# A one-core fp32 layer: weight-sum copies issued by another engine, a product's order, an eviction order, and two banks for the last block

## The chip, the cores and the metric

The kernel runs on one core of a Trainium2 chip. The metric is the device time of one execution in microseconds (us). A core has a tensor engine (PE, with its weight loads shown apart as PEld), a vector engine (DVE), a scalar engine (ACT), GpSimd (POOL) and a sync engine (SP), which mostly issues DMA transfers. Each engine takes its instructions in order and waits on semaphores for the others; transfers run on 16 DMA engines that all issuers share. Two of the DMA queues matter: q1, filled by SP and ACT, and q0, filled by POOL.

## The reference

One layer of a diffusion backbone over 1024 tokens of 1024 channels, all in fp32:

```python
hx = _modulate(_rmsnorm(x, norm1_g[l]), sh1, sc1)          # and hc, 256 context tokens
o_na  = _na_latent(...)                                    # neighbourhood attention + context keys
o_ret = _ret_output(_bi_retention(...), xrg)               # chunked retention, both directions
    # step: scores = (q k^T) * dmat ; out = scores v + (q state) * xi
    #       state = g_chunk * state + (k*zeta)^T v         (context tokens give the first state)
x = x + g1 * _merge(o_na, o_ret, xga, xgb, w_proj_na, w_proj_ret, w_out)
hx2 = _modulate(_rmsnorm(x, norm2_g[l]), sh2, sc2)
u = conv3(hx2 @ w_up) + conv_b ; a, val = split(u)          # 2 x 2816 columns
x = x + g2 * ((silu(a) * val) @ w_down)                    # 2816 -> 1024
return _rmsnorm(x, final_norm_g)
```

## The kernel before

**Products.** Every fp32 product is three products of a faster format: each operand is split into a high part (a cast, on ACT, line 95) and a low part (the rest, a subtraction, mostly on DVE, line 96), and PE multiplies hi by hi, hi by lo and lo by hi into one bank. `mm3` (L129 to L132) does this for one product, `open3` (L1421 to L1423) for one of a chain.

**The feed-forward part** uses a scheme with seven block products in place of eight. For that, sums of quarter blocks are needed, of the weights and of the activations. The up products run in units (class `Seven`, L1425), of 7 steps each; a unit's weight sums s1 to s4 are made on POOL (L1432 to L1435), cast on ACT and used by PE.

The down product is seven passes in a row: A11·B11, S2·T2, A12·B21, S3·T3, S1·T1, A22·T4, S4·B22, each over 11 steps j (a step is one `operands` pair, L2268, and 12 matmuls of 128x512 outputs, `steps`, L2289). The A and S are 512-column pieces of the activations, kept in DRAM as `d_a`; the T are sums of blocks of the down weights, kept in DRAM as `d_w`. They are made while the up products run:

- The activations: `conv` writes A11, A22, A12 and first copies of the S with SP's stores `d_a<-at` (L1981 and, for the second half of the blocks, L1986). Then POOL's accumulating transfers (`act_sum`, L1993, `d_a<-d_a`) do S3 += A11, S1 += A22, S2 += S1, S4 += S2 for each j, each after the one before it that it reads has landed.
- The weights: `block_sums` (L555) yields 88 calls for 11 jobs of 4 sums: 44 copies from the weights to `d_w` (`copy_of`, L560, transfers of 16x4096 elements issued by SP at L562) and 44 accumulating transfers on POOL (`sum_of`, L564, issued at L558). The order within a round is copy 0 of job n, sum 0 of job n-1, copy 2, sum 3 of job n-2, copy 1, sum 2 of n-1, copy 3, sum 1 of n-1. A sum waits for its copy; sum 1 waits for sum 0, and sum 3 for sum 1.

Both are put into the stream of the up units by hand: after steps 1 and 3 of a unit, `puts` (L592) has POOL copy one column of a result of that unit (`pad<-pu`, L593), which holds POOL until the step is there, then come two calls of `block_sums` and one of `act_sum`. What is left after the last unit is drained: first all of `block_sums`, then all of `act_sum` (L2250 to L2252). `late` keeps these instructions in program order; a scheduler places the others.

**Loads of the down product.** All operands of all passes are one stream of loads on SP's queue (`ur_load`, L2145 to L2147; 12 buffers, 8 loads ahead): `ur<-d_a` and `ur<-d_w` or `ur<-in_w_down`. A load waits for the sum it reads and holds every later one on SP. The copies L562 stand on SP between these loads and the activation stores.

**Retention.** For each of 4 heads, `front` computes q, k, v of a block of 128 tokens (blocks 0 and 1 are the context) into a bank, which is evicted: v's high part by ACT (L1165), its low part by DVE (L1166), and for context blocks k (`r`) by ACT (L1170). `state` scales k to `kz` (ACT L1199, DVE L1200) for the product dS. In `mix_a`, the product Q of q with two running states SS is one `mm3` (L1245); SS's high part is cast on ACT (L1230) and its low part made on POOL (L1231).

**The end.** In the last pass (p = 6), the first 7 of 11 steps are run for four blocks b = 0 to 3 together; the last four are run block by block under a written-out order (L2375 to L2404), each block ending with a scale and a subtraction on DVE (L2392, L2393), a sum of squares on ACT (L2395), a factor on POOL (L2310, L2311), a scaling on ACT and DVE (L2316, L2317) and a store. Block 3 does this in two halves of 256 columns, one after the other, in the same bank.

Of the kernel before, what the change touches and what calls it, by code (L numbers as in the profile page):

```python
# [8 lines left out]
F32 = mybir.dt.float32  # L9
F32R = mybir.dt.float32r  # L10
AF = mybir.ActivationFunctionType
ALU = mybir.AluOpType
# [4 lines left out]
P = 128  # L17
D = 1024
# [4 lines left out]
NCB = C // P  # L23
# [17 lines left out]
def tile_hybrid_layer(ctx, tc: tile.TileContext, io, dbg=None):  # L41
# [87 lines left out]
    def mm3(out, ah, al, bh, bl, first, last):  # L129
        pe.matmul(out, ah, bh, start=first, stop=False)  # L130
        pe.matmul(out, ah, bl, start=False, stop=False)  # L131
        pe.matmul(out, al, bh, start=False, stop=last)  # L132
# [419 lines left out]
    NH, EARLY, PRE = NF // 2, 4, 8  # L552
    seq = [j + NH * i for j in range(NH) for i in range(2)]

    def block_sums(jobs):  # L555

        def add(out, src):
            late(pool.dma_start(out, src, accum_op=ALU.add, max_dma_last_dim=8192))  # L558

        def copy_of(n, c):  # L560
            d, x, y, z, w = jobs[n]
            late(sync.dma_start(d[c], (y, z, z, w)[c]))  # L562

        def sum_of(n, c):  # L564
            d, x, y, z, w = jobs[n]
            add(d[c], (x, d[0], y, d[1])[c])

        jobs = list(jobs)
        for n in range(len(jobs) + 2):
            for f, m, c in ((copy_of, n, 0), (sum_of, n - 1, 0), (copy_of, n, 2), (sum_of, n - 2, 3), (copy_of, n, 1), (sum_of, n - 1, 2), (copy_of, n, 3), (sum_of, n - 1, 1)):  # L570
                if 0 <= m < len(jobs):
                    yield f(m, c)
# [14 lines left out]
    def down_jobs(j0, j1):  # L587
        for j in range(j0, j1):
            b = {(r, c): io["w_down"][c, NH * r + j] for r in range(2) for c in range(2)}
            yield [d_w[j, c] for c in range(4)], b[0, 0], b[0, 1], b[1, 1], b[1, 0]  # L590
# [539 lines left out]
    class Head:  # L1130
# [21 lines left out]
        def front(self, i):  # L1152

            src, tb = (hcp, i) if i < NCB else (hxp, self.order[i - NCB])
            c0 = P if i < NCB else 0
            m = mm_tile()
            for n, kb in enumerate(self.kbs):
                xh, xl = src(0, kb, tb * P, P), src(1, kb, tb * P, P)
                w = self.wr[kb]
                mm3(m[:, c0:512], xh, xl, w[:, 0, c0:512], w[:, 1, c0:512], n == 0, n == KB - 1)  # L1160
                if n in (2, 5):
                    yield
            vtag = f"c{i}" if i < NCB else tb
            self.v[i] = v = rt.tile([P, 2, DV], F32R, tag=f"v{vtag}", bufs=1, name="v")
            act.copy(v[:, 0], m[:, 256:512])  # L1165
            vec.tensor_tensor(v[:, 1], m[:, 256:512], v[:, 0].bitcast(F32), ALU.subtract)  # L1166
            r0 = rt.tile([P, 2, 2, 2, 32], F32, tag="r0", bufs=2, name="r0")
            self.r0[i] = r0f = r0.rearrange("p q a t i -> p q (a t i)")
            if i < NCB:
                act.copy(r0f[:, 1], m[:, P : 2 * P])  # L1170
                return
            r1 = rt.tile([P, 2, 2, 2, 32], F32, tag="r1", bufs=2, name="r1")
            mv = m[:, 0:256].rearrange("p (q a t i) -> p q a t i", q=2, a=2, t=2)
            for a, ti in ((0, tb), (1, NTB)):
                cs = cosT[:, ti, 0].unsqueeze(1).unsqueeze(1).to_broadcast([P, 2, 2, 32])
                sn = cosT[:, ti, 1].unsqueeze(1).to_broadcast([P, 2, 32])
                vec.tensor_tensor(r0[:, :, a], mv[:, :, a], cs, ALU.mult)
                vec.scalar_tensor_tensor(r1[:, :, a, 0], mv[:, :, a, 1], -1.0, sn, ALU.mult, ALU.mult)
                vec.tensor_tensor(r1[:, :, a, 1], mv[:, :, a, 0], sn, ALU.mult)
            pool.tensor_tensor(r0f, r0f, r1.rearrange("p q a t i -> p q (a t i)"), ALU.add)  # L1180
# [43 lines left out]
        def mix_a(self, n):  # L1224
            tb = self.back[n]
            q, k = self.qk[tb][:, :, 0], self.qk[tb][:, :, 1]
            run = self.run
            SS = rt.tile([P, 2, 2, DV], F32R, tag="SS", bufs=1, name="SS")
            for i, s in ((self.ci, self.sts[tb]), (self.oi, run)):
                act.copy(SS[:, 0, i], s)  # L1230
                pool.tensor_tensor(SS[:, 1, i], s, SS[:, 0, i].bitcast(F32), ALU.subtract)  # L1231
            if n + 1 < NTB:
                self.run = rt.tile([P, DV], F32, tag="run", bufs=2, name="run")
                vec.scalar_tensor_tensor(self.run, run, self.dec(4 + self.oi), self.dss[tb], ALU.mult, ALU.add)
            Ap = prt.tile([P, 2, P], F32, tag="s", bufs=2, name="Ap")
            pe.matmul(Ap, k[:, 0], q, start=True, stop=False, skip_group_check=True)
            pe.matmul(Ap[:, 0], k[:, 1], q[:, 0], start=False, stop=True, skip_group_check=True)
            A0 = rt.tile([P, 2, P], F32, tag="A0", bufs=1, name="A0")
            self.A[n] = A = rt.tile([P, 2, P], F32R, tag="Ahl", bufs=2, name="A")
            vec.tensor_tensor(A0, Ap, Dm[:, self.h].unsqueeze(1).to_broadcast([P, 2, P]), ALU.mult)  # L1240
            vec.tensor_tensor(A0[:, 0], A0[:, 0], A0[:, 1], ALU.add)
            split(A[:, 0], A[:, 1], A0[:, 0])
            Q = prt.tile([P, 2, DV], F32, tag="w", bufs=2, name="Q")
            SSf = SS.rearrange("p l i v -> p l (i v)")
            mm3(Q.rearrange("p i v -> p (i v)"), q[:, 0], q[:, 1], SSf[:, 0], SSf[:, 1], True, True)  # L1245
            self.o[n] = o = rt.tile([P, DV], F32, tag="o", bufs=3, name="o")
            act.activation(o, Q[:, 0], AF.Copy, scale=self.dec(2))
            vec.scalar_tensor_tensor(o, Q[:, 1], self.dec(3), o, ALU.mult, ALU.add)
# [172 lines left out]
    def open3(out, ah, al, bh, bl, first, last):  # L1421
        for n, (a, b) in enumerate(((ah, bh), (ah, bl), (al, bh))):
            pe.matmul(out, a, b, start=first and n == 0, stop=last and n == 2, skip_group_check=True)  # L1423
# [808 lines left out]
    cb = tap.tile([P, 2 * NF], F32, name="cb")  # L2232
    sync.dma_start(cb, io["conv_b"])
    units = [u0 if n == 0 else Later(opening[n]) if n < EARLY else Up(n, j) for n, j in enumerate(seq)]
    dn_sums = block_sums(down_jobs(0, NH))
    order, at = [], 0
    for i in range(NF):
        nk = 7 if i >= EARLY else 4 if opening[i].whole else 5
# [46 lines left out]
    def gs(dh):  # L2285
        return slice(dh * 512, dh * 512 + 512)
# [3 lines left out]
    def steps(p, js, first, last):  # L2290
        g = p % 2
        for j in js:
            a, w = operands(p, j)
            for b in range(QB):
                ts = slice(b * P, (b + 1) * P)
                open3(banks[g][b], a[:, 0, ts], a[:, 1, ts], w[:, 0], w[:, 1], first and j == 0, last and j == NH - 1)

    part = {}

    def square(tb, dh, junk):  # L2300
        act.activation(junk, part[tb, dh], AF.Square, accum_out=ssf[:, tb, dh : dh + 1])
# [19 lines left out]
    def finish(tb, dh):  # L2321
        factor(tb, dh)
        scaled(tb, dh)
# [50 lines left out]
    steps(6, range(NH - NL), False, False)  # L2374
    with tc.manual_schedule():  # L2375
        tl = [operands(6, j) for j in range(NH - NL, NH)]
        for b in range(QB):
            ts = slice(b * P, (b + 1) * P)
            z, junk = dw_tile("z", 6), dw_tile("xr", 4)
            part[b, 1] = z  # L2380
            last = b == QB - 1
            parts = (slice(0, 256), slice(256, 512)) if last else (slice(0, 512),)
            for c in parts:
                for i, (a, w) in enumerate(tl):
                    open3(banks[0][b][:, c], a[:, 0, ts], a[:, 1, ts], w[:, 0, c], w[:, 1, c], False, i == NL - 1)
            if b == 0:
                for tb in range(NTB - 3, NTB):
                    finish(tb, 0)
            if last:
                factor(b - 1, 1)  # L2390
            for n, c in enumerate(parts):
                vec.tensor_tensor(z[:, c], banks[0][b][:, c], gate2[:, 512 + c.start : 512 + c.stop], ALU.mult)  # L2392
                vec.tensor_tensor(z[:, c], p1[b][:, c], z[:, c], ALU.subtract)  # L2393
                k = 5 if n else 1
                act.activation(junk[:, c], z[:, c], AF.Square, accum_out=ssf[:, b, k : k + 1])  # L2395
                if last and not n:
                    s = ssf[:, b]
                    pool.tensor_scalar(s[:, 2:3], s[:, 1:2], 1.0 / D, s[:, 2:3], ALU.mult, ALU.add)
            if last:
                scaled(b - 1, 1)  # L2400
            elif b:
                finish(b - 1, 1)
        factor(QB - 1, 5)
        scaled(QB - 1, 1)  # L2404
    pd[1].release()
# [111 lines left out]
```

## Time and profile before

| what | value |
| --- | --- |
| time, median of 3 runs | 1713.4 us (1713.31 to 1713.5) |
| time of the profiled execution | 1713.02 us |
| its span in the trace | 1710.8 us |
| mean granted TensorE clock | 0.997 |
| PE, DVE, ACT, POOL busy | 99%, 73%, 49%, 32% |
| hardware queue q1, software queue q0 | 47.0% and 21.7% of 16 engines' span |

Times in the trace are in us from the span's start; the execution's own time is 2.2 us longer than the span. A row of the timeline has start, duration, engine, line, operation, destination and sources, a count of like instructions in a row, and in brackets the idle time before it with what ended it. The table of waits has an engine's instruction, the instruction it waited for, the sum of the waits in us, their number and the longest. "SPq" is SP's sequencer issuing transfers.

### The profile page before, as it was taken

To read this page: it belongs to the slowest core of one execution; us is meant where nothing else is said; L and a number is where in the kernel's file an instruction comes from. 1 tells how busy PE (TensorE), PEld (TensorE's weight loads), DVE (VectorE), ACT (ScalarE), POOL (GpSimd) and SP (SyncE) were. 2 spreads that over 40 slices of the span, in tenths; PEclk is the share of its full clock that TensorE was granted. 3 is DMA by queue.
4 is the path that set the end of the run, shared out by engine and by line. 5 is a ranking of instruction groups with operands and counts; after the bars stand their busy time and mean duration, and the time that the engine had idled before them with its cause. 6 is when DMAs were issued, how large, how long until landed. Compare 5 with 4: busy or idle time off the path is not lost. (4 is left out here: it accounts for less than half of the span.)

```text
span 1710.8 us, 25367 instructions
## 1 busy us (share of the span) xinstructions
PE 1689.3 (99%) x8365; PEld 1410.8 (82%) x8365; DVE 1256.1 (73%) x2481; ACT 843.3 (49%) x1777; POOL 551.9 (32%) x697
## 2 busy tenths in 40 slices
PE   9999999999999999999999999999999999998998
PEld 7788888888888887888888888888888888877886
DVE  5777786665787877567557876897888988836756
ACT  6565665553444434353446444754444444534444
POOL 2101233322344354013320221014566655211444
PEclk9999999999999999999999999999999999999999
DMA  9255789863465643899989976886676667988744
GB/s 381 94 150 165 180 204 226 215 176 66 134 163 136 191 87 99 264 330 333 305 219 314 251 225 205 276 264 190 194 196 184 167 199 192 262 251 300 241 158 174
DMA packets 171459, 357.65 MB, mean 209 GB/s; under 512 B 30656, under 2 KB 47584, under 8 KB 163968
## 3 DMA queue, kind: packets, MB, share of 16 engines
q1 hardware_dynamic: 135856, 274.91, 47.0%
q0 software_dynamic: 20864, 66.18, 21.7%
q10 hardware_dynamic: 14608, 14.95, 2.6%
q8 instruction: 66, 1.08, 0.3%
q14 instruction: 65, 0.53, 0.1%
HBM read 279.62 MB, written 150.26 MB: 251 GB/s over the span
## 5 line engine op out<-in xcount | busy, mean ns | idle before, releaser
L1423 PE MATMUL u<-T,wc 128*128 128x512 f32 x1056 | 246.4, 389 | 0.3 <-DVE T L96 0.2
L1423 PEld LDWEIGHTS u<-T,wc 128*128 128x128 f32 x1056 | 198.0, 188 | 42.3 <-DVE T L96 0.6
L1423 PE MATMUL y<-wc,ahl 128*128 128x512 f32 (+1 forms) x936 | 212.7, 389 | 6.0 <-ACT wc L95 5.6
L1423 PEld LDWEIGHTS y<-wc,ahl 128*128 128x128 f32 x936 | 175.5, 189 | 43.3 <-ACT wc L95 6.0
L96 DVE TENSOR_TENSOR wc<-ur,wc 128x512 fp32r<-128x512 f32 x171 | 128.4, 755 | 46.1 <-ACT wc L95 44.4
L95 ACT CAST wc<-ur 128x512 fp32r<-128x512 f32 x171 | 105.5, 621 | 105.5 <-PE u L1423 53.8
L120 PE MATMUL mm<-low,wc 128*128 128x512 f32 (+1 forms) x312 | 119.1, 382 | 0.0
L1423 PE MATMUL u<-h2a,wc 128*128 128x512 f32 x504 | 118.2, 389 | 0.0
L1423 PEld LDWEIGHTS u<-h2a,wc 128*128 128x128 f32 x504 | 94.5, 188 | 19.6
L119 PE MATMUL mm<-hx,wc 128*128 128x512 f32 x264 | 107.3, 407 | 0.3 <-ACT hc L233 0.3
L121 PE MATMUL mm<-hx,wc 128*128 128x512 f32 x264 | 104.8, 397 | 0.0
L534 POOL DMA_DIRECT2D d_ona<-rs x32 | 32.1, 1004 | 221.8 <-DVE st L495 61.5
L593 POOL COPY pad<-pu 128x1 f32<-128x1 f32 x62 | 38.6, 622 | 159.6 <-DVE pu L1464 117.6
L1423 PE MATMUL u<-hxT,wc 128*128 128x512 f32 x384 | 90.0, 389 | 0.0
L1423 PEld LDWEIGHTS u<-hxT,wc 128*128 128x128 f32 x384 | 72.1, 188 | 15.0
L96 DVE TENSOR_TENSOR ahl<-ur,ahl 128x512 fp32r<-128x512 f32 x66 | 52.5, 801 | 33.0 <-ACT ahl L95 32.9
L95 ACT CAST wc<-wr 128x512 fp32r<-128x512 f32 x69 | 42.7, 621 | 67.1 <-PE u L1423 53.9
L132 PE MATMUL mm<-wc,low 128*128 128x512 f32 (+1 forms) x180 | 68.9, 383 | 0.0
L95 ACT CAST wc<-s 128x512 fp32r<-128x512 f32 x56 | 34.8, 622 | 68.6 <-PE u L1423 66.4
L95 ACT CAST wc<-raw 128x512 fp32r<-128x512 f32 x77 | 47.9, 622 | 36.5 <-PE u L1423 5.6
L120 PEld LDWEIGHTS mm<-low,wc 128*128 128x128 f32 x312 | 59.1, 189 | 7.2
L1423 PE MATMUL u<-hx,wc 128*128 128x512 f32 x192 | 62.3, 390 | 0.0
(438 smaller groups left out, 4585.0 us busy)
## 6 DMA issues: line engine op xcount, KB each, us to landing
d_a<-at SPq DMA_DIRECT2D x77, 256.0 KB, 5.4
ur<-d_a SPq DMA_DIRECT2D x77, 256.0 KB, 5.3
ur<-in_w_up SPq DMA_DIRECT2D x76, 256.0 KB, 6.2
aw<-in_w_ada SPq DMA_DIRECT2D x32, 512.0 KB, 4.9
d_w<-in_w_down SPq DMA_DIRECT2D x44, 256.0 KB, 7.4
d_a<-d_a POOLq DMA_DIRECT2D x44, 256.0 KB, 7.0
ur<-d_w SPq DMA_DIRECT2D x44, 256.0 KB, 4.1
ur<-in_w_down SPq DMA_DIRECT2D x33, 256.0 KB, 5.4
```

The source lines that it names most:

```text
L95: act.copy(hi, src)
L96: (lo_eng or vec).tensor_tensor(lo, src, hi.bitcast(F32), ALU.subtract)
L119: pe.matmul(out, wh, xh, start=k == 0, stop=False)
L120: pe.matmul(out, wh, xl, start=False, stop=False)
L121: pe.matmul(out, wl, xh, start=False, stop=k == n - 1)
L132: pe.matmul(out, al, bh, start=False, stop=last)
L534: late(pool.dma_start(o, self.rs[HD:P], accum_op=ALU.add))
L593: late(pool.tensor_copy(tick, src))
L1423: pe.matmul(out, a, b, start=first and n == 0, stop=last and n == 2, skip_group_check=True)
```

## The change

Four edits:

1. The 44 copies of the down weights' sums are issued by POOL in place of SP. They stay in `block_sums`' own order among POOL's sums.
2. In head 0, for the context blocks, the evictions of v's high part and of k on ACT are kept in program order.
3. The product Q takes its three parts in the order hi·hi, lo of q by hi of SS, hi of q by lo of SS.
4. In the last pass, block 3's sum over the first 7 steps is closed and taken over (scaled and subtracted into `rest`) after block 0; its last four steps go, half by half, to two banks of their own of the other group.

```diff
-    def block_sums(jobs):
+    def block_sums(jobs, eng=None):
...
-            late(sync.dma_start(d[c], (y, z, z, w)[c]))
+            late((eng or sync).dma_start(d[c], (y, z, z, w)[c]))
...
-            act.copy(v[:, 0], m[:, 256:512])
+            pin = late if self.h == 0 and i < NCB else lambda ins: ins
+            pin(act.copy(v[:, 0], m[:, 256:512]))
...
-                act.copy(r0f[:, 1], m[:, P : 2 * P])
+                pin(act.copy(r0f[:, 1], m[:, P : 2 * P]))
...
-            mm3(Q.rearrange("p i v -> p (i v)"), q[:, 0], q[:, 1], SSf[:, 0], SSf[:, 1], True, True)
+            for i, (a, b) in enumerate(((0, 0), (1, 0), (0, 1))):
+                pe.matmul(Q.rearrange("p i v -> p (i v)"), q[:, a], SSf[:, b], start=i == 0, stop=i == 2)
...
-    dn_sums = block_sums(down_jobs(0, NH))
+    dn_sums = block_sums(down_jobs(0, NH), pool)
...
-                open3(banks[g][b], a[:, 0, ts], a[:, 1, ts], w[:, 0], w[:, 1], first and j == 0, last and j == NH - 1)
+                open3(banks[g][b], a[:, 0, ts], a[:, 1, ts], w[:, 0], w[:, 1], first and j == 0, j == (NH if last else NH - NL if p == 6 and b == QB - 1 else 0) - 1)
...
+            if b == QB - 1:
+                break
...
+            if b == 0:
+                rest = p1[QB - 1]
+                vec.tensor_tensor(u2[QB - 1], banks[0][QB - 1], gate2[:, gs(1)], ALU.mult)
+                vec.tensor_tensor(rest, rest, u2[QB - 1], ALU.subtract)
+            else:
                 factor(b - 1, 1)
...
+                if b < QB - 2:
+                    scaled(b - 1, 1)
+        ends = [pd[1].tile([P, 512], F32, tag="y", bufs=4, name="y")[:, 0:256] for _ in halves]
+        for bank, c in zip(ends, halves):
+            for i, (a, w) in enumerate(tl):
+                open3(bank, a[:, 0, ts], a[:, 1, ts], w[:, 0, c], w[:, 1, c], i == 0, i == NL - 1)
+        factor(b - 1, 1)
+        for n, (bank, c) in enumerate(zip(ends, halves)):
+            vec.tensor_tensor(z[:, c], bank, gate2[:, 512 + c.start : 512 + c.stop], ALU.mult)
+            vec.tensor_tensor(z[:, c], rest[:, c], z[:, c], ALU.subtract)
...
+            if not n:
...
+                scaled(b - 2, 1)
+        scaled(b - 1, 1)
```

Where the copies stand, on SP, at the end of the up products. Before, each row a transfer that SP issues (`xN` is N in a row; 128x512 is one operand, 16x4096 one copy):

```order
606 L2147 DMA ur<-d_w 128x512
607 L2147 DMA ur<-d_a 128x512
608 L1986 DMA d_a<-at 128x512 x3
609 L562 DMA d_w<-in_w_down 16x4096 x3
610 L2147 DMA ur<-d_w 128x512
611 L2147 DMA ur<-d_a 128x512
```

and the same place after:

```order
557 L2149 DMA ur<-d_a 128x512
558 L2149 DMA ur<-d_w 128x512
559 L1988 DMA d_a<-at 128x512 x3
560 L2149 DMA ur<-d_a 128x512
561 L2149 DMA ur<-d_w 128x512
562 L2149 DMA ur<-d_a 128x512
```

The three last copies no longer stand behind the last stores of activations, and the loads close up.

POOL at the same time, from the last `pad` to the end of the drain. Before (`d_w<-d_w` is sum 1 or 3, `d_w<-in_w_down` sum 0 or 2):

```order
595 L558 DMA d_w<-d_w 32x2048
596 L1993 DMA d_a<-d_a 32x2048
597 L558 DMA d_w<-in_w_down 32x2048
598 L558 DMA d_w<-d_w 32x2048
599 L558 DMA d_w<-in_w_down 32x2048
600 L558 DMA d_w<-d_w 32x2048
601 L558 DMA d_w<-in_w_down 32x2048
602 L558 DMA d_w<-d_w 32x2048
603 L558 DMA d_w<-in_w_down 32x2048
604 L558 DMA d_w<-d_w 32x2048 x2
605 L1993 DMA d_a<-d_a 32x2048 x6
```

and after, with the copies as rows of L562:

```order
632 L558 DMA d_w<-d_w 32x2048
633 L562 DMA d_w<-in_w_down 16x4096
634 L1995 DMA d_a<-d_a 32x2048
635 L558 DMA d_w<-in_w_down 32x2048
636 L562 DMA d_w<-in_w_down 16x4096
637 L558 DMA d_w<-d_w 32x2048
638 L562 DMA d_w<-in_w_down 16x4096
639 L558 DMA d_w<-in_w_down 32x2048
640 L562 DMA d_w<-in_w_down 16x4096
641 L558 DMA d_w<-d_w 32x2048
642 L558 DMA d_w<-in_w_down 32x2048
```

The four copies of the last job now stand on POOL, between the sums of the job before, and ahead of all the sums that read them.

DVE at the end of the kernel, from block 2 on (`z` is a block's result, `y` a bank, `pd` an SBUF tile). Before:

```order
2299 L2392 TENSOR_TENSOR z<-y,gate_15575 128x512
2300 L2393 TENSOR_TENSOR z<-pd,z 128x512
2301 L2317 SCALAR_TENSOR_TENSOR z<-z,ssf,fg 128x512
2302 L2392 TENSOR_TENSOR z<-y,gate_15575 128x256
2303 L2393 TENSOR_TENSOR z<-pd,z 128x256
2304 L2392 TENSOR_TENSOR z<-y,gate_15575 128x256
2305 L2393 TENSOR_TENSOR z<-pd,z 128x256
2306 L2317 SCALAR_TENSOR_TENSOR z<-z,ssf,fg 128x512 x2
```

and after:

```order
2301 L2391 TENSOR_TENSOR z<-y,gate_15575 128x512
2302 L2392 TENSOR_TENSOR z<-pd,z 128x512
2303 L2408 TENSOR_TENSOR z<-y,gate_15575 128x256
2304 L2409 TENSOR_TENSOR z<-pd,z 128x256
2305 L2319 SCALAR_TENSOR_TENSOR z<-z,ssf,fg 128x512
2306 L2408 TENSOR_TENSOR z<-y,gate_15575 128x256
2307 L2409 TENSOR_TENSOR z<-pd,z 128x256
2308 L2319 SCALAR_TENSOR_TENSOR z<-z,ssf,fg 128x512 x2
```

The first half of block 3 moves ahead of block 1's scaling. On PE, the rows of before and after differ only in Q's order and in the bank of block 3.

More of the change, by code (lines that the diff above doesn't have):

```diff
@@ L2376, in tile_hybrid_layer @@
         tl = [operands(6, j) for j in range(NH - NL, NH)]
+        halves = (slice(0, 256), slice(256, 512))
         for b in range(QB):
@@ L2380, in tile_hybrid_layer @@
             part[b, 1] = z
[L2381 to L2385, printed above, removed]
+            if b == QB - 1:
+                break
+            for i, (a, w) in enumerate(tl):
+                open3(banks[0][b], a[:, 0, ts], a[:, 1, ts], w[:, 0], w[:, 1], False, i == NL - 1)
             if b == 0:
@@ L2388, in tile_hybrid_layer @@
                     finish(tb, 0)
-            if last:
-                factor(b - 1, 1)
[L2391 to L2402, printed above, removed]
+            vec.tensor_tensor(z, banks[0][b], gate2[:, gs(1)], ALU.mult)
+            vec.tensor_tensor(z, p1[b], z, ALU.subtract)
+            square(b, 1, junk)
+            if b == 0:
[3 more added lines that the diff above has]
+            else:
+                factor(b - 1, 1)
+                if b < QB - 2:
+                    scaled(b - 1, 1)
+        ends = [pd[1].tile([P, 512], F32, tag="y", bufs=4, name="y")[:, 0:256] for _ in halves]
+        for bank, c in zip(ends, halves):
+            for i, (a, w) in enumerate(tl):
+                open3(bank, a[:, 0, ts], a[:, 1, ts], w[:, 0, c], w[:, 1, c], i == 0, i == NL - 1)
[3 more added lines that the diff above has]
+            vec.tensor_tensor(z[:, c], rest[:, c], z[:, c], ALU.subtract)
+            k = 5 if n else 1
+            act.activation(junk[:, c], z[:, c], AF.Square, accum_out=ssf[:, b, k : k + 1])
+            if not n:
+                s = ssf[:, b]
+                pool.tensor_scalar(s[:, 2:3], s[:, 1:2], 1.0 / D, s[:, 2:3], ALU.mult, ALU.add)
+                scaled(b - 2, 1)
+        scaled(b - 1, 1)
         factor(QB - 1, 5)
```

## Prediction

> **What bounds the kernel now.** I read the page's busy times first, then PE's waits, then the timeline of each engine around the largest wait, and last the windows of the up products and the end.
>
> ```profile
> PE 1689.3 (99%) x8365; PEld 1410.8 (82%) x8365; DVE 1256.1 (73%) x2481; ACT 843.3 (49%) x1777; POOL 551.9 (32%) x697
> ```
>
> PE is the bound nearly everywhere: 1689.3 of 1710.8 us. An edit that removes no matmul can gain only where PE waits or runs at a lower clock. From PE's waits, the longest and the one that edit 3 touches (total, times, longest):
>
> ```profile
> PE y L1423 <- ACT wc L95: 5.6, 1, 5.6
> ...
> PE Q L131 <- POOL SS L1231: 1.2, 4, 0.5
> ```
>
> The first is a single hole. PE's timeline around it, and the window just behind it (PE busy, PEld, DVE, ACT, POOL, then the granted clock):
>
> ```profile
> 1529.76 8.78 PE L1423 MATMUL y<-wc,ahl 128*128 128x512 f32 x38
> 1544.09 6.07 PE L1423 MATMUL y<-wc,ahl 128*128 128x512 f32 x15 [5.55 <-ACT wc L95]
> ```
>
> ```profile
> 1544.00:1546.00 2.00, 1.89 (x4) 1.20 (x5) 0.84 (x2) 0.44 (x2) 0.00 (x0) 0.50 0.94 341
> ```
>
> The first row gives the pace: 38 matmuls in 8.78 us, of which the last takes about 0.39 to finish, so (8.78 - 0.39) / 37 = 0.227 us each. Without the hole, the 53 matmuls of both rows would take 53 x 0.227 + 0.16 = 12.2 us; they take 1550.16 - 1529.76 = 20.4. So the hole costs **8.2 us**: 5.55 idle and 2.7 more because the clock stands at 0.50 when PE starts again.
>
> Who is late? ACT cast the operand only when its load had come, SP issued that load late, and POOL had issued the sum late that the load reads:
>
> ```profile
> 1542.90 0.62 ACT L95 CAST ahl<-ur 128x512 fp32r<-128x512 f32 x1 [14.30 <-DMA ur<-d_a]
> ```
>
> ```profile
> 1484.89 0.63 SPq L562 DMA_DIRECT2D d_w<-in_w_down  x1
> ...
> 1499.02 1.61 SPq L1986 DMA_DIRECT2D d_a<-at  x3
> 1502.16 3.06 SPq L562 DMA_DIRECT2D d_w<-in_w_down  x3
> ...
> 1524.78 0.32 SPq L2147 DMA_DIRECT2D ur<-d_a  x1
> ...
> 1540.16 0.32 SPq L2147 DMA_DIRECT2D ur<-d_a  x1
> ```
>
> ```profile
> 1479.42 1.36 POOL L558 DMA_DIRECT2D d_w<-in_w_down  x1
> ...
> 1488.44 0.77 POOL L558 DMA_DIRECT2D d_w<-d_w  x1 [4.40 <-issue]
> 1496.04 0.77 POOL L558 DMA_DIRECT2D d_w<-in_w_down  x1 [6.83 <-DMA d_w<-in_w_down]
> ...
> 1508.94 0.77 POOL L558 DMA_DIRECT2D d_w<-in_w_down  x1 [11.34 <-DMA d_w<-in_w_down]
> 1509.66 0.86 POOL L558 DMA_DIRECT2D d_w<-d_w  x1
> 1517.76 0.78 POOL L558 DMA_DIRECT2D d_w<-d_w  x1 [7.23 <-DMA ur<-d_a]
> 1518.42 0.92 POOL L1993 DMA_DIRECT2D d_a<-d_a  x1
> 1525.13 2.36 POOL L1993 DMA_DIRECT2D d_a<-d_a  x3 [5.79 <-DMA d_a<-d_a]
> 1536.36 0.77 POOL L1993 DMA_DIRECT2D d_a<-d_a  x1 [8.87 <-DMA d_a<-d_a]
> ```
>
> Read backwards: the load of 1540.16 needs the sum S2 of the last j, issued at 1536.36; that stands on POOL behind the weight sums, the last at 1517.76; these waited 6.83 and 11.34 us for copies. The last three copies were issued by SP at 1502.16, right behind the three stores of activations at 1499.02. The copies wait for nothing themselves: their place on SP holds them. The chain is copy, weight sum, activation sum, load, cast, PE.
>
> **Edit 1, the copies on POOL.** It takes 44 issues from SP and puts 44 on POOL. For the last job: its four copies now stand between the sums of the job before, the first one right behind the sum ahead of 1479.42, the last one ahead of 1488.44.
>
> ```profile
> L562 SPq DMA_DIRECT2D d_w<-in_w_down x44: 489/514/1252, 1110.2 to 1504.7; - x44
> ...
> DMA to landing us min/median/max: 2.9/7.4/10.6
> ```
>
> POOL's price of an issue is bounded by its neighbours at 0.77 (1488.44) and 1.36 (1479.42); I take 0.8, since the form is close and most rows say 0.77. Four copies are 3.2 us, partly inside the 4.40 us wait. So the row of 1488.44 moves to about 1490 (1488.4 to 1491.6). The sum of 1496.04 follows at 1491, as its copy is then 11 us old and lands in 7.4 to 10.6. The next links wait for each other's landing, which took 1517.76 - 1509.66 = 8.1 us: job 9's sum 3 at 1498, job 10's sum 2 and sum 1 at 1499 and 1500, its sum 3, the last, at 1508. That is 9.8 us earlier than 1517.76. From the last weight sum to PE's restart, before took 1544.09 - 1517.76 = 26.3 us (two landings of activation sums, a load, a cast); I keep that. PE's operand is ready at 1534.3. PE wants it at 1529.76 + 38 x 0.227 = 1538.4. So the hole closes with some 4 us to spare, and with it the half clock: **-8.2 us**. What is late next is the loads behind it; they followed the load of 1540.16 without a wait on sums, so they move forward too. The issues that SP loses were beside PE's work and save nothing by themselves.
>
> What edit 1 may cost is in the up products, where POOL also makes the units' weight sums:
>
> ```profile
> 1110.00:1484.00 374.00, 373.94 (x1650) 309.26 (x1650) 327.16 (x353) 178.64 (x247) 186.38 (x170) 1.00 0.72 202
> ```
>
> ```profile
> L1433 POOL TENSOR_TENSOR s<-s,ur x14: 1283/2151/2164, 1188.5 to 1439.8; 128x512 f32<-128x512 f32 x14
> ```
>
> ```profile
> 1346.56 1.62 POOL L1433 TENSOR_TENSOR s<-s,ur 128x512 f32<-128x512 f32 x1
> ```
>
> ```profile
> 1353.67 0.62 ACT L95 CAST wc<-s 128x512 fp32r<-128x512 f32 x1 [2.15 <-PE u L1423]
> ```
>
> PE never waits there (373.94 of 374), and POOL is busy half of it (186.38). A unit's first needed sum ends at 1348.18 and is cast at 1353.67, when PE has freed the tile: 5.5 us of slack, the smallest I found. Two copies a unit are 1.6 us. I take **nothing**, hidden by that slack; queueing behind the copies could use it up (a rival below).
>
> **Edit 3, Q's low part last.** PE waits four times, 1.2 us in all, for SS's low part, which is made on POOL behind the cast. The low part is now wanted one matmul later, 0.227 us, so at most 4 x 0.227 = **-0.9 us**, between 0 (if the third product's operand is then late for another reason) and 1.2. All three matmuls remain.
>
> **Edit 2, the context evictions.**
>
> ```profile
> 373.33 0.27 ACT L1170 COPY r<-mm 128x128 f32<-128x128 f32 x1
> ```
>
> ```profile
> 373.66 0.50 PE L130 MATMUL mm<-wc,hx 128*128 128x512 f32 x1 [0.63 <-ACT r L1170]
> ```
>
> PE's next product waits 0.63 us for the bank, until ACT has copied k of block 0 behind the second v. With k first it can go as soon as its own product and v's other reader on DVE are done. I take **-0.5 us** (0 to 1): no more than this wait, and part of it may go to the next reader.
>
> **Edit 4, the last block.**
>
> ```profile
> 1697.79 4.84 PE L1423 MATMUL y<-wc,ahl 128*128 128x512 f32 x32
> ```
>
> ```profile
> 1702.67 0.42 DVE L2392 TENSOR_TENSOR z<-y,gate 128x256 f32<-128x256 f32 x1 [0.79 <-PE y L1423]
> ...
> 1703.47 0.42 DVE L2392 TENSOR_TENSOR z<-y,gate 128x256 f32<-128x256 f32 x1
> ```
>
> PE ends at 1702.63, and only then DVE begins with the first half, since both halves share a bank. In a bank of its own the first half can be read before, and behind PE's end stand only two DVE instructions instead of four: 1703.47 - 1702.67 = 0.8 us at most. Block 1's scaling now stands between the halves and may delay the second by some 0.2. I take **-0.6 us** (0.3 to 0.8). The two added instructions after block 0 lie beside PE's work.
>
> **Sum.** 8.2 + 0.9 + 0.5 + 0.6 = 10.2 us. The profiled execution took 1713.02 (span 1710.8, 2.2 outside it), the median of the runs 1713.4. So 1702.8 against the one and 1703.2 against the other; I give **1703.2**. A measurement of this kernel tells a change from none at about 0.2%, 3.4 us.
>
> **The rivals.**
>
> *The hole shrinks but stays* (0.18). The margin is 4 us after five links (two landings of weight sums, two of activation sums, a load) of 3 to 9 us each. Landings of copies spread from 2.9 to 10.6 us, and the copies now run beside POOL's own sums. If five links are 1.2 to 1.8 us longer each, 2 to 5 us of idle time remain, with up to 2.7 for the clock: 1705 to 1711. For it: the DMA engines are loaded around there (share 0.94 in the window above), and POOL issues one by one. Against it: before's links already ran among these loads. [...]
>
> *The hole stays* (0.10). Then it isn't the place on SP but the landing of the copies or the chain of sums that sets the time: POOL still waits for its copies, and the drain ends near 1517. Only edits 2 to 4 count: 1713.4 - 2.0 = 1711.4. For it: POOL waits for a DMA at nearly each step of the drain. Against it: SP issued the last copies 17 us after the one of 1484.89, and behind the stores. [...]
>
> *Slower: POOL falls behind in the up products* (0.06). Its place is the units' weight sums L1432 to L1435, which stand on POOL behind the transfers of the unit before. POOL waits for a DMA in order; if a sum's landing is put off by a copy ahead of it in the same queue by 7.4 us, the weight sums come 1.6 + 7.4 = 9.0 us later. The point from which it decides is 5.5 us of slack: 3.5 us lost at the tightest unit. Over the 14 units with such sums (the x14 of L1433), at half of that, 1.75 x 14 = 24.5 us, less the 10.2: about 1718. Against it: POOL is idle for half of that stage, and copies are issued two places or more ahead of what reads them.
>
> *Edits 2 to 4 do nothing* (0.08): 1713.4 - 8.2 = 1705.2.
>
> **How the numbers follow.** My forecast has the remaining 0.58. The forecast's own range is 1701.5 to 1705: lower with 1.2, 1.0 and 0.8 for the small edits and another 0.7 for what I may have missed beside them. To hold 8 in 10, the range reaches to most of the shrunk hole: 1701.5 to 1709. Faster by over 0.2% (below 1710.0) are the forecast, nearly all of the shrunk hole and the last rival: 0.82. Within: the hole that stays, and some of the slow case: 0.12. Slower: 0.06.
>
> **What would show it.** Right: no wait of PE over 1 us in the down product, the granted clock at 1.00 all through 1530 to 1560; POOL's last weight sum near 1508 and no wait of sums for copies; PE still busy for all of the up products. Edit 4: DVE's first half begins before PE's end, and the time from PE's last matmul to the end is 0.3 to 0.8 us shorter. Edit 3: PE's waits for SS L1231 gone or below 0.3 us. Wrong: a wait PE y <- ACT in pass two at any later time, sums of POOL that still wait over 5 us for `d_w<-in_w_down`, or new waits PE u <- ACT wc in the up products.

## The result, and the profile after

The changed kernel took 1703.51 us (median of 4 runs, 1702.45 to 1704.71) against 1713.36 us for the kernel before on the same chip (4 runs, 1711.29 to 1713.5): a ratio of 0.9946, interval 0.9928 to 0.9963, or 9.3 us less (6.3 to 12.3). The forecast was 1703.2. The profiled execution took 1704.71 us with a span of 1702.9.

The hole is gone. PE's waits of the changed kernel begin with the old small ones, and none for the down product's operands is left but 0.4 us for DVE; PE's timeline across the place is a single row:

```profile
PE c L203 <- POOL ident masks.py:199: 1.4, 1, 1.4
PE R L522 <- DVE PT L507: 1.2, 1, 1.2
PE dS L132 <- DVE kz L1201: 0.9, 2, 0.5
...
PE Q L1247 <- POOL SS L1232: 0.6, 3, 0.2
...
PE y L1425 <- DVE wc L96: 0.4, 1, 0.4
```

```profile
1519.62 40.74 PE L1425 MATMUL y<-wc,ahl 128*128 128x512 f32 x179
```

The same stretch as a window (its length, then the busy time and count of instructions of PE, PEld, DVE, ACT and POOL, the granted clock, the share of the DMA engines, GB/s), of before and of after:

```profile
1484.00:1560.00 76.00, 70.43 (x301) 57.48 (x300) 37.97 (x55) 31.69 (x55) 12.39 (x16) 0.96 0.91 281
```

```profile
1484.00:1560.00 76.00, 76.00 (x337) 62.92 (x337) 47.50 (x67) 36.79 (x62) 17.94 (x20) 1.00 0.98 309
```

In the same 76 us PE now runs 337 matmuls in place of 301: 36 more, at 0.227 us each 8.2 us. POOL's drain shows how:

```profile
1480.12 0.77 POOL L562 DMA_DIRECT2D d_w<-in_w_down  x1
...
1486.18 1.06 POOL L562 DMA_DIRECT2D d_w<-in_w_down  x1
1489.33 0.77 POOL L558 DMA_DIRECT2D d_w<-d_w  x1 [2.09 <-DMA d_w<-in_w_down]
1489.84 1.05 POOL L558 DMA_DIRECT2D d_w<-in_w_down  x1
1496.00 0.77 POOL L558 DMA_DIRECT2D d_w<-d_w  x1 [5.11 <-DMA d_w<-d_w]
...
1506.86 0.77 POOL L558 DMA_DIRECT2D d_w<-d_w  x1 [7.45 <-DMA d_w<-d_w]
...
1523.76 0.77 POOL L1995 DMA_DIRECT2D d_a<-d_a  x1 [7.04 <-DMA ur<-d_w]
```

The last job's copies are issued between 1480.12 and 1486.18 (before: 1484.89 to 1504.7). The waits of 6.83 and 11.34 us for copies are gone; the long waits that are left are of sums for sums (5.11 and 7.45). The last weight sum is issued at 1506.86 in place of 1517.76. The late operand is loaded and cast well before PE asks for it, 88 matmuls behind the row's start, at 1519.62 + 88 x 0.227 = 1539.6. ACT's row of the weight that goes with it:

```profile
1533.15 0.62 ACT L95 CAST wc<-ur 128x512 fp32r<-128x512 f32 x1
```

It is cast by 1533.77, so 5.8 us are to spare.

The end, DVE's rows of the changed kernel from block 3's first half on. PE's last matmul ends at 1695.60, by its row:

```profile
1687.81 7.79 PE L1425 MATMUL y<-wc,ahl 128*128 128x512 f32 x45
```

```profile
1694.20 0.42 DVE L2408 TENSOR_TENSOR z<-y,gate 128x256 f32<-128x256 f32 x1
1694.66 0.43 DVE L2409 TENSOR_TENSOR z<-pd,z 128x256 f32<-128x256 f32 x1
1695.01 0.75 DVE L2319 SCALAR_TENSOR_TENSOR z<-z,ssf,fg 128x512 f32<-128x512 f32 x1
1695.67 0.42 DVE L2408 TENSOR_TENSOR z<-y,gate 128x256 f32<-128x256 f32 x1
1696.12 0.42 DVE L2409 TENSOR_TENSOR z<-pd,z 128x256 f32<-128x256 f32 x1
```

The first half is read 1.4 us before PE ends, and the second begins 0.07 us after it; before, it began 0.84 us after (1703.47 against 1702.63).

**A table by stage.** Single runs of one kernel scatter by 2 to 5 us (the kernel before: 1710.1 to 1715.6 in the later comparisons), too much for the small edits. So PE's 8365 matmuls are numbered by their start, and each trace gives the time between the starts of two numbers (7600 to 7700 are 100 matmuls around the hole: 22.7 us at 0.227 each), and from PE's end to the span's end. us:

| kernel | 2000 to 2600, context | 2600 to 3900, retention | 5800 to 7600, up products | 7600 to 7700, hole | after PE's end |
| --- | --- | --- | --- | --- | --- |
| before | 110.90 | 252.29 | 408.36 | 30.89 | 8.16 |
| after | 110.74 | 252.79 | 408.35 | 22.67 | 7.30 |
| copies only | 110.95 | 253.00 | 408.35 | 22.67 | 7.97 |
| all but the copies | 110.82 | 251.40 | 408.34 | 29.11 | 7.42 |
| copies on ACT | 110.84 | 251.86 | 408.94 | 23.34 | 7.40 |
| last four copies | 110.93 | 253.35 | 408.36 | 22.67 | 8.30 |
| last four earlier on SP | 110.92 | 253.08 | 408.35 | 22.67 | 8.46 |
| 7 additions at the drain | 110.96 | 252.34 | 408.34 | 24.79 | 7.27 |
| 11 additions at the drain | 110.85 | 251.71 | 408.36 | 28.61 | 7.29 |
| 7 additions a unit | 110.79 | 252.79 | 472.30 | 22.67 | 7.28 |
| 3 additions a unit | 111.18 | 251.83 | 431.72 | 22.67 | 7.31 |
| Q's order only | 110.93 | 251.45 | 408.35 | 30.53 | 8.14 |
| copies in four parts | 110.79 | 250.80 | 408.37 | 22.67 | 7.29 |

### The profile page after: what moved, and what is told of

Its sections match the earlier page's. It is cut to its first block, busy times and chain, and to the rows that moved or that the text cites. A ratio compares the mean times of both kernels' runs of the same rounds, so it can differ in the third digit from the quotient of the medians.

```text
span 1702.9 us, 25380 instructions
## 1 busy us (share of the span) xinstructions
PE 1687.3 (99%) x8365; PEld 1409.0 (83%) x8365; DVE 1261.2 (74%) x2483; ACT 844.6 (50%) x1777; POOL 573.5 (34%) x741
## 5 line engine op out<-in xcount | busy, mean ns | idle before, releaser
L96 DVE TENSOR_TENSOR wc<-raw,wc 128x512 fp32r<-128x512 f32 x77 | 54.8, 720 | 11.9 <-ACT wc L95 11.2
```

What stands on the lines that cost most here:

```text
L96: (lo_eng or vec).tensor_tensor(lo, src, hi.bitcast(F32), ALU.subtract)
```

## The experiments

Ratios are to the kernel before, in runs on the same chip, with 95% intervals.

### The copies alone

(`block_sums` takes the engine as in the change.)

```diff
-    dn_sums = block_sums(down_jobs(0, NH))
+    dn_sums = block_sums(down_jobs(0, NH), pool)
```

> The kernel before with the first edit alone (44 copies issued by POOL, in the same order). If the place of the copies on SP made the hole, as predicted: the wait PE y <- ACT wc is gone, the clock stays at 1.00 from 1530 to 1560 us, and the time falls by 8.2 us, to about 1705.0; PE's waits for SS and the time from PE's last matmul to the end (8.2 us) stay as before. If a good part of the 9.9 us came from the other three edits: 1707 or more, with the hole still partly there.

Measured: 1705.16 us against 1712.39, 0.9957 (0.9944 to 0.9971), 7.4 us less (5.0 to 9.6). In the trace the hole is gone altogether: 22.67 in place of 30.89, 8.2 us. PE's waits for SS stay (1.4 us in 5 places), and so does the end (7.97).

### All but the copies

```diff
-    dn_sums = block_sums(down_jobs(0, NH), pool)
+    dn_sums = block_sums(down_jobs(0, NH))
```

> The changed kernel with the 44 copies back on SP, so edits 2 to 4 alone. By the prediction 2.0 us less than before, 1711.4: 0.9 from Q's order, 0.5 from the context, 0.6 at the end, and the hole stays as it was, 5.5 us and the half clock. If the small edits do nothing outside the end, 1712.5 to 1713. If they were what closed the hole: near 1704.

Measured: 1710.70 against 1712.39, 0.9990 (0.9982 to 0.9999), 1.7 us less (0.2 to 3.1). The hole stays. PE's timeline there:

```profile
1527.68 9.68 PE L1425 MATMUL y<-wc,ahl 128*128 128x512 f32 x42
1541.23 10.97 PE L1425 MATMUL y<-wc,ahl 128*128 128x512 f32 x37 [3.87 <-ACT wc L95]
```

and the clock stands at 0.50 for 3.4 us, where before it did for 6.8:

```profile
1541.34:1544.75 3.41, 3.33 (x7) 2.26 (x8) 0.64 (x2) 0.30 (x1) 0.00 (x0) 0.50 0.85 275
1544.75:1548.20 3.45, 3.31 (x15) 2.38 (x14) 2.59 (x4) 2.16 (x5) 0.00 (x0) 1.00 1.03 389
```

So it costs 29.11 - 22.67 = 6.4 us in this trace, not 8.2: the hole's price isn't the same in every trace.

### The copies on ACT

```diff
-    dn_sums = block_sums(down_jobs(0, NH), pool)
+    dn_sums = block_sums(down_jobs(0, NH), act)
```

> The changed kernel with the 44 copies issued by ACT in place of POOL, through the same hardware queue q1 as SP's copies. If only the place behind the stores of activations on SP matters, the hole is gone here too and the time is within 1 us of the changed kernel, 1703 to 1704.5; ACT's own casts are late by no more than the 0.5 us of an issue. If POOL's queue, or that POOL issues a copy right where it needs it, is what matters, the hole stays at least partly: over 1706, with sums on POOL waiting over 5 us for d_w<-in_w_down.

Measured: 1704.84 against 1712.39, 0.9955 (0.9943 to 0.9968), a little over the 1703 to 1704.5 that was expected. The expectation has the queue wrong, and so has the description of the queues at the start: ACT's transfers don't go through q1. The rows of the queues, of before and then of this kernel, show 11.5 MB, the size of the 44 copies, leaving q1 for q10:

```profile
q1 hardware_dynamic: 135856, 274.91, 47.0%
q10 hardware_dynamic: 14608, 14.95, 2.6%
```

```profile
q1 hardware_dynamic: 134448, 263.38, 45.7%
q10 hardware_dynamic: 16016, 26.48, 4.5%
```

So this run changes the engine, its queue and the place at once; it shows that POOL's own queue isn't needed, as the wait for the operand is gone, and leaves it to the run with the copies earlier on SP to tell the place from the queue. PE loses 0.6 us in the up products and 0.7 at the place of the hole; and POOL still waits for copies, which ACT issues late, as they stand behind its other work:

```profile
1493.81 7.35 ACTq L562 DMA_DIRECT2D d_w<-in_w_down  x3
```

```profile
1499.87 0.77 POOL L558 DMA_DIRECT2D d_w<-in_w_down  x1 [3.37 <-DMA d_w<-in_w_down]
1504.29 0.79 POOL L558 DMA_DIRECT2D d_w<-d_w  x1 [3.65 <-DMA d_w<-in_w_down]
1510.70 0.78 POOL L558 DMA_DIRECT2D d_w<-d_w  x1 [5.62 <-DMA d_w<-d_w]
```

The drain ends at 1510.70, between before (1517.76) and after (1506.86).

### Only the last four copies on POOL

```diff
-            late(sync.dma_start(d[c], (y, z, z, w)[c]))
+            late((eng if eng and n == NH - 1 else sync).dma_start(d[c], (y, z, z, w)[c]))
```

> The kernel before with only the four copies of the last of 11 jobs issued by POOL; the other 40 stay on SP, and edits 2 to 4 are left out. If it is the four copies that stood behind the last stores, this alone closes the hole: the same time as with all 44 on POOL within 1 us, about 1705.0. If SP had to be freed of all the copies, or the earlier ones count too, the hole is only smaller: 1707 to 1712.

Measured: 1704.92 against 1712.39, 0.9955 (0.9943 to 0.9968); the hole is gone (22.67). Four of 44 copies carry all of the first edit's gain.

### The last four copies earlier on SP

```diff
+            if ahead and n == NH - 1 and not early:
+                return
             late(sync.dma_start(d[c], (y, z, z, w)[c]))
...
         for n in range(len(jobs) + 2):
+            if ahead and n == NH - 2:
+                for c in (0, 2, 1, 3):
+                    copy_of(n + 1, c, True)
```

> The kernel before, all 44 copies still issued by SP, but the four of the last job one round (two units) earlier in SP's order, ahead of the stores of activations that they stood behind; the number of calls and POOL's order stay. If the place on SP made the hole, and not the issuing engine or its queue, this closes it as well: no wait PE y <- ACT wc, 100 matmuls around the place in 22.7 us in place of 30.9, about 1705. If the hole goes only when another engine issues: 1712 to 1713, as before.

Measured: 1705.30 against 1712.08, 0.9964 (0.9952 to 0.9977), and the hole is gone (22.67), with no edit but the place on SP's own queue. SP issues them at 1447:

```profile
1447.11 3.14 SPq L564 DMA_DIRECT2D d_w<-in_w_down  x5
```

and POOL's last weight sum is issued as in the changed kernel:

```profile
1506.78 0.78 POOL L558 DMA_DIRECT2D d_w<-d_w  x1 [7.63 <-DMA ur<-d_w]
```

This settles the cause: the place of four copies, not the engine that issues them or its queue. The transfers' own time isn't what decides: from issue to landing a copy took 7.4 us in the median before and 7.4 here, where the hole is gone, and 4.8 on ACT, whose drain ended later than here. Nor is the gain of 8.2 us the time of the issues, since SP issues all 44 here: what another engine saved was a place in SP's order.

### A delay at the drain: how much is to spare, and what a short hole costs

```diff
     for _ in dn_sums:
         pass
+    for _ in range(7):
+        late(pool.tensor_tensor(idle, idle, idle, ALU.add))
     act_sum(len(act_sums))
```

> The changed kernel with 7 idle additions of 128x512 on POOL (1.29 us each, 9.0 in all) between the last weight sum and the drained activation sums; nothing reads them. In the trace of the changed kernel the late operand is cast by 1533.8 and wanted at 1539.6, so 5.8 us are to spare, and a delay of 9.0 leaves 3.2 us of idle time: the time goes up by 3.2 if a short hole costs only itself, by 4.9 if the clock is halved for one span of 3.4 us as in the trace of the kernel without the first edit (3413 ns at 0.50 there), to 1706.7 or 1708.4. If the spare time is more than 9 us, nothing is lost: 1703.5.

Measured: 1707.09 against 1712.08, 0.9972 (0.9963 to 0.9981). By the ratios that is 4.5 us more than the changed kernel (0.9946); the raw medians, which come from two chips, differ by 3.6. The execution in the trace was the quickest of the eleven (1705.35 of 1705.35 to 1709.61); it loses 2.1 us there (24.79), with the clock at 1.00 from 1539.50 to 1546.30, around the wait, and what the others lost isn't seen. The late operand itself came in time; the wait is for the first operand of the next pass:

```profile
1542.23 0.51 PE L1425 MATMUL y<-wc,ahl 128*128 128x512 f32 x1 [1.20 <-ACT wc L95]
1543.05 9.17 PE L1425 MATMUL y<-wc,ahl 128*128 128x512 f32 x39 [0.32 <-DVE wc L96]
```

The second run has 11 additions.

> As the one before with 11 additions, 14.2 us. 5.8 to spare leave 8.4 us of idle time; with the clock at half for two spans of 3.4 us (6827 ns at 0.50 in the trace of before) the loss is 8.4 + 3.4 = 11.8, to 1715.3; with one such span 10.1, with none 8.4. If later loads catch up only slowly after such a delay, more than 12.

Measured: 1708.91 against 1712.08, 0.9986 (0.9977 to 0.9995); by the ratios 6.9 us more than the changed kernel, and 5.9 us lost in the trace (28.61), where 8.4 to 11.8 were expected. POOL's rows:

```profile
1504.25 15.95 POOL L2254 TENSOR_TENSOR idle<-idle 128x512 f32<-128x512 f32 x11
1520.14 0.78 POOL L1995 DMA_DIRECT2D d_a<-d_a  x1
```

PE's timeline, and the windows around:

```profile
1525.79 12.18 PE L1425 MATMUL y<-wc,ahl 128*128 128x512 f32 x53
1540.47 0.50 PE L1425 MATMUL y<-wc,ahl 128*128 128x512 f32 x1 [2.51 <-ACT wc L95]
```

```profile
1538.10:1541.50 3.40, 0.72 (x2) 0.41 (x3) 1.29 (x2) 1.14 (x2) 0.00 (x0) 1.00 0.95 283
1541.50:1544.90 3.40, 3.40 (x9) 2.63 (x9) 0.00 (x0) 0.37 (x1) 0.00 (x0) 0.50 0.99 318
```

From the first drained activation sum to PE's restart it takes 1540.47 - 1520.14 = 20.3 us, where the kernel before took 1544.09 - 1518.42 = 25.7: the chain behind the drain was shorter here, where it started later, and so the delay cost less than itself. Why it was shorter is not shown: the DMA engines' share over the chain was 0.70 in the kernel before and 0.78 with seven additions, where it took 22.6 us, so a lighter load beside it doesn't explain it. And the clock stood at 0.50 from 1541.50 to 1544.90, behind a wait of 2.51 us: PE was busy for 0.72 of the 3.40 us before.

### More work for POOL in the up products

The first kernel puts seven additions of a tile that nothing else uses into each unit, the second three; the third has none, and issues each copy in four parts.

```diff
             puts(dn_sums, (units[i].u2 if n == 1 else units[i].u3)[:, 0:1], 2)
             act_sum(1)
+            for _ in range(4 if n == 1 else 3):
+                late(pool.tensor_tensor(idle, idle, idle, ALU.add))
```

> The changed kernel with idle additions of 128x512 on POOL in the up products, behind the transfers of each step: four after a unit's step 1, three after its step 3, 7 x 1.29 = 9.0 us a unit, the delay that the slow rival took. If 5.5 us of slack decides, PE waits for weight sums in most units and some 24 us are lost, about 1728. If POOL's present idle time in that stage (186 of 374 us busy) swallows them, since POOL waits for pad and for landings anyway: 0 to 3 us, 1703.5 to 1706.5, and the drain may begin later and eat from the 5.8 us to spare.

Measured: 1768.44 against 1712.08, 1.0331 (1.0317 to 1.0345): 65 us more than the changed kernel, 64 of them in the up products (472.30 against 408.35). Neither theory had that. PE waits for DVE, not for weight sums:

```profile
PE u L1425 <- DVE pu L1472: 30.5, 15, 3.1
PE u L1425 <- DVE pu L1466: 8.7, 10, 4.0
```

POOL was busy for 336 of 374 us there, nearly full, so this alone doesn't tell POOL's lateness from a slower DVE. The next two do:

```diff
-            for _ in range(4 if n == 1 else 3):
+            for _ in range(2 if n == 1 else 1):
```

> As the run with idle additions in the up products, but three a unit (two behind step 1, one behind step 3), 3 x 1.45 = 4.4 us a unit. In that run a unit took 22.7 us in place of 19.0 with POOL and DVE both at work for nearly all of it, so POOL's own share is about 22.7 - 10.2 = 12.5 to 13.7 us a unit and 5.3 to 6.5 are spare. If a threshold decides (spare time of POOL per unit), 4.4 us fit and nothing is lost: 1703.5 to 1705. If additions on POOL cost by slowing DVE (its rows were up to twice as long beside them), the loss is in proportion, 65 x 3 / 7 = 28 us, about 1731.

Measured: 1727.68 against 1713.08, 1.0088 (1.0072 to 1.0103), 24 us over the changed kernel, 23.4 of them in the up products; in proportion, 28 were expected, and 0 if spare time decided. POOL has time left (280 of 374 us). DVE's subtractions for the units' sums, first in the changed kernel, then here (shortest, median, longest in ns):

```profile
L96 DVE TENSOR_TENSOR wc<-s,wc x56: 676/694/1776, 1203.2 to 1469.8; 128x512 fp32r<-128x512 f32 x56
```

```profile
L96 DVE TENSOR_TENSOR wc<-s,wc x54: 674/1181/2650, 1204.4 to 1480.5; 128x512 fp32r<-128x512 f32 x54
```

The median goes from 694 to 1181 ns. DVE was busy for 328 of 374 us there in the changed kernel and is for 354 now, and PE waits for it: 12.5 us in all. The rest lies mostly in the last unit, with one wait of 5.6 us for a cast on ACT, and the mean granted clock is 0.997 against 0.999 in the changed kernel; so the loss is not spread evenly, and its closeness to 28 is in part chance.

```diff
-            late((eng or sync).dma_start(d[c], (y, z, z, w)[c]))
+            src = (y, z, z, w)[c]
+            if eng is None:
+                late(sync.dma_start(d[c], src))
+                return
+            for r in range(4):
+                late(eng.dma_start(d[c][32 * r : 32 * r + 32], src[32 * r : 32 * r + 32]))
```

> The changed kernel with each of the 44 copies issued by POOL in four parts of 32 rows, so 132 more issues and the same bytes. At 0.47 to 0.77 us each that is 2.8 to 4.6 us more a unit on POOL, with no additions that slow DVE. If POOL has spare time for issues in the up products, nothing is lost there (408.4 us for matmuls 5800 to 7600, as in all kernels so far), and the drain, 12 issues longer, takes up to 9 us of the 5.8 to spare: 1703.5 to 1707. If POOL's lateness by over some 3 us a unit reaches PE: 10 us or more lost, over 1713.

Measured: 1703.59 against 1713.08, 0.9948 (0.9935 to 0.9962), the same as the changed kernel. The window of the up products:

```profile
1110.00:1484.00 374.00, 373.90 (x1650) 309.33 (x1649) 326.43 (x354) 178.82 (x247) 266.14 (x335) 1.00 0.74 203
```

POOL is busy 60 us more than in the changed kernel (266.14 against 206.27), not much less than the 74 of the run before, and PE loses nothing: 408.37. DVE's subtractions keep their median:

```profile
L96 DVE TENSOR_TENSOR wc<-s,wc x56: 678/693/2493, 1201.0 to 1467.5; 128x512 fp32r<-128x512 f32 x56
```

So 60 us more of POOL's time in issues cost nothing here and left DVE's median at 693 ns; 74 us more in additions cost 23.4 us, with the median at 1181 ns.

### Q's order alone

```diff
-            mm3(Q.rearrange("p i v -> p (i v)"), q[:, 0], q[:, 1], SSf[:, 0], SSf[:, 1], True, True)
+            for i, (a, b) in enumerate(((0, 0), (1, 0), (0, 1))):
+                pe.matmul(Q.rearrange("p i v -> p (i v)"), q[:, a], SSf[:, b], start=i == 0, stop=i == 2)
```

> The kernel before with the order of Q's three products alone changed. By the prediction 0.9 us less, within what the runs scatter (1710 to 1715); the trace decides: PE's waits for SS fall from 1.2 to 1.7 us in 4 to 6 places to below 0.9 in 3, and matmuls 2600 to 3900, which hold the retention (252.3 to 253.4 us in four traces with the old order), take 251.4 to 252.8. If the order does nothing: 252.3 to 253.4 and waits of over 1 us.

Measured: 1711.21 against 1713.08, 0.9989 (0.9980 to 0.9998), 1.9 us less (0.3 to 3.4). In the trace the waits fall as expected:

```profile
PE Q L1246 <- POOL SS L1231: 0.6, 3, 0.2
```

The retention takes 251.45. Over all the traces, the four kernels with the old order have 252.3 to 253.4 (mean 252.9), the nine with the new one 250.8 to 252.8 (mean 251.9): 1.0 us.

## Why the prediction was right, point by point

The sum was 10.2 us; the traces give 8.2 + 1.0 + 0.1 + 0.9 = 10.2, and the medians 9.85. That the two sums agree to a tenth is luck: the context gave 0.4 less than forecast, and the end and Q's order 0.4 more. A further 0.4 us that no term of the prediction had lies outside the span: the executions of the three kernels that have the last four copies late on SP take 2.2 us longer than their spans, all others 1.7 to 1.9, also with 11 additions, which have a hole. So it goes with the place of the copies; no trace covers that time, and its cause stays open. And one pair of traces wouldn't have shown the sum: the spans of before and after differ by 7.9 us only, since the changed kernel's trace took 0.9 us more up to matmul 2000 and 0.5 more in the retention, no more than such stages scatter from trace to trace (324.05 to 325.25 us up to matmul 2000, where the kernels are alike).

- **The hole** (-8.2): right in mechanism and size. Seven kernels close it and show 22.67 us for the hundred matmuls; the one with only four copies moved, and the one that leaves them on SP but earlier, show that their place in SP's order was the cause. "The copies wait for nothing themselves" was not quite so. SP's waits from 1480 to 1510 in the kernel before have the loads ahead of the copies waiting for stores to land, and two waits of the copies themselves:

```profile
SPq L2147 <- DMA d_a<-at: 6.8, 6, 4.8
...
SPq L562 <- DMA ur<-d_a: 1.5, 1, 1.5
SPq L562 <- DMA ur<-d_w: 1.4, 1, 1.4
```

  So the place was one behind waiting loads as well as behind stores, and 2.9 us were the copies' own. The chain was forecast to end at 1508 on POOL; it was 1506.86 (1 us less), and 4 us were to be spare; it was 5.8. The 26.3 us from there to PE, which the working kept, were 26.9 in the changed kernel (1506.86 to 1533.77). Counted from the first drained activation sum, 25.7 and 26.2 became 20.3 when the drain was delayed by 11 additions, so the figure can't be moved far. The hole's price isn't fixed either: 8.2, 6.4 and 7.9 us in the traces of three kernels that have it, with 5.55, 3.87 and 4.59 us without a matmul. The clock was at half for 6.8 us in the first and 3.4 in the second; for the third it isn't shown.
- **Copies in the up products at no cost**: right. 408.35 us against 408.36, and POOL's busy time rose by 206.27 - 186.38 = 19.9 us, 0.47 for each of the 42 copies there, less than the 0.8 that was taken. They go out in a row about 0.5 us apart.
- **Q's order** (-0.9): right, 1.0 (PE's waits for SS, the part that the working named, fell by 0.6 of it, from 1.2 to 0.6), though a run's scatter in that stage is as large; the changed kernel's own trace (252.79) would not have shown it.
- **The context** (-0.5): mis-sized; 0.1 or less (110.93 in the mean of the five old traces, 110.87 of the eight new). The step "with k first it can go as soon as its own product and v's other reader on DVE are done" was right, but that reader ends late, so the wait it counted on saving is mostly kept. ACT's and PE's rows of the changed kernel:

```profile
374.07 0.27 ACT L1171 COPY r<-mm 128x128 f32<-128x128 f32 x1 [0.49 <-DVE v L1167]
```

```profile
374.39 0.50 PE L130 MATMUL mm<-wc,hx 128*128 128x512 f32 x1 [0.51 <-ACT r L1171]
```

  k now waits for DVE in place of ACT's second v, and PE's wait goes from 0.63 to 0.51 us.
- **The end** (-0.6, 0.3 to 0.8): a little more, 0.9: from PE's end to the last instruction 8.21 us in the mean of five traces without the edit, 7.32 in eight with it. The two instructions of 0.8 us that the working took as the most are nearly all of it; the five traces themselves lie between 7.97 and 8.46. Block 1's scaling between the halves did not delay the second one (it began 0.07 us after PE's end).
- **The rival of a shrunk hole**: it did not happen. Its price for a chain that comes late was too high: a delay of 9.3 us cost 2.1 in its trace and 4.5 by the ratios, one of 16.0 cost 5.9 and 6.9, since 5.8 us were to spare in place of 4 and the chain shrank. Its price for idle time was not: the 5.9 us came with waits of 2.51 and twice 0.3 us. As for the clock, it stayed at 1.00 around a wait of 1.20 us and stood at 0.50 for 3.4 us behind one of 2.51.
- **The slow rival**: it did not happen, and its mechanism was not the one that would have made it. With additions on POOL, PE's waits were for DVE's instructions that read its banks and, once in each of the two kernels, for a cast on ACT; none was for weight sums. POOL took 132 issues more at no cost (408.37 us in the up products); three additions a unit cost 23.4 us there, with DVE's median at 1181 ns in place of 694.

## What to carry to other kernels

When one late operand makes a hole, follow its chain back to the first transfer that waits for nothing, and look at what stands ahead of it on its queue: moving four of 44 copies, to another engine or only to an earlier place on the same one, was worth as much as moving all. Work out how much is to spare behind a repaired hole, and take the landings in that working from the same traffic, since here the chain behind the drain went from 25.7 us to 20.3 when it was moved. Before giving an engine more to do, ask what kind of work it is: here 60 us more on POOL cost nothing as issues, and 74 us more cost 23 as additions.

## What was not expected of the hardware

- With additions of 128x512 on POOL, DVE's subtractions beside them took longer: a median of 1181 ns with three a unit, in place of 694. With 132 more DMA issues on POOL, 60 us of its time against 74, it was 693.
- The clock didn't answer every hole alike. In the kernel before, PE was busy for 0.04 of the 5.50 us from 1538.50 to 1544.00, and the clock stood at 0.50 for 6.8 us, till between 1548 and 1550. In the one without the first edit, with a wait of 3.87 us, it stood at 0.50 from 1541.34 to 1544.75, with PE busy for 3.33 us of these 3.41, and was back at 1.00 behind them. With 11 additions and a wait of 2.51 us, PE was busy for 0.72 of the 3.40 us up to 1541.50, and the clock stood at 0.50 for the next 3.40. With 7 additions and a wait of 1.20 us, PE was busy for 2.03 of the 3.40 us around it, and the clock stayed at 1.00. What decides between these is not shown.
- A chain of accumulating transfers and loads, from the first drained activation sum to the cast operand, took 3 to 6 us less where it was started later (25.7 and 26.2 us without a delay, 22.6 and 20.3 with one).
